# Wider warm-up matmuls, TensorE transposes for two more head tiles, and weights in K thirds in a list-scheduled head

## Chip, cores, metric

One core of one Trainium2 chip. The metric is the device time of one execution in microseconds. Kernel before: 389.12 us (median of 6 runs, 388.9 to 389.19).

## The reference

```python
x: (8, 1024, 768) f32;  gamma: (768,) f32;  w_qkv: (768, 2304) f32
rms = sqrt(mean(x**2, axis=-1) + eps)
out = matmul(x / rms * gamma, w_qkv)          # (8, 1024, 2304) f32
```

## The kernel before

The 8192 rows are 64 tiles of 128. `gamma` is folded into the weights when they are converted to bf16, `1/rms` is applied when an accumulator is evicted, so a tile needs: its load, a bf16 transposed copy `xT` (768 x 128 as six blocks), and per 512 output columns six accumulating matmuls. The first six tiles ("head") run while the weights still arrive; their order on every engine is a list of (time, operation) made in advance by a list scheduler. The rest is a loop, ordered by planned times too. Every operation is issued in that order; times only sort.

```python
PIECES = [(0, 2, 0, 512), ..., (0, 3, 512, 512), (3, 6, 512, 512), ...]   # weight loads: K chunks k0..k1, columns n0, n
LOADS  = [..., (-8.86, "x", 5), (16.69, "t", 4), (16.70, "w", 9), (21.71, "t", 5), ...]   # w piece, x tile, t: DMA transpose
HEAD_PLAN = [(4.99, "conv", 0, 0, "ACT"), ..., (5.95, "trA", 0), ..., (8.59, "mm", 0, 0, "01"), ...]
    # conv: weight chunk to bf16   trA/trB: fp32 TensorE transposes of tiles 0 to 2 (4 and 2 blocks), cpA/cpB their copies
    # tr/cp: bf16 transposes and copy (tile 3)   mm tile, column, K chunks   evac: eviction   stat, recip: row statistic

    def idle(n):                                  # warm-up matmuls
        wps = psum.tile([P, P], f32, name="pm")
        for _ in range(n):
            nc.tensor.matmul(out=wps, lhsT=warm, rhs=warm, start=True, stop=True)

    at(0.0, idle, 18)
    at(2.8, gamma_in)
    at(2.81, idle, 28)
    ...
    for t in range(HEAD, MT):                     # the steady part
        ahead = 6.0 if t < HEAD + 5 else 0.0
        at(now - 15 - ahead, load_x, t)           # unless it is in LOADS
        at(now - 8.5 - ahead, cast, t)
        at(now - 7.5 - ahead, xbar, t)            # DMA transpose of the bf16 tile into xT
        ...
```

## Time and profile before

| | before |
|---|---|
| median time | 389.12 us |
| span of the profiled run | 387.34 us |
| first real matmul starts | 8.70 us |
| last real matmul starts | 383.28 us |
| of that stretch, waits and transposes | 0.92 us, 0.34 us |

TensorE (PE in the profile) is busy nearly all the time, so whatever the other engines do is free unless TensorE waits for it. The prediction below shows the lines that say so. Times inside a run are from the start of its span. A *real* matmul is one of the product, not of the warm-up and not a transpose; a *step* is the time from the start of one to the start of the next, and it is too long by what it has over 0.216 us (0.109 us for 256 columns) and over the time of any transposes in it. The *fetch* is the transfer of a 16 KB packet of instructions, which shares the DMA engines with the loads; where no other is named, it is the first of a run. "Landed" times are those at which a load's semaphore is complete in the trace. Weight pieces are counted from 0 in the order of `PIECES`; in the kernel before piece 6 is K chunks 3 to 5 of columns 512 to 1023, in the changed kernel pieces 5, 6 and 7 share those columns, two chunks each.

### The profile page before, as it was taken

What the parts mean: (1) busy time and instruction counts of PE and PEld (TensorE: products, weight loads), DVE (VectorE), ACT (ScalarE), POOL (GpSimd) and SP (SyncE); (2) the same over time, 40 slices, a digit from 0 to 9 for tenths busy, and PEclk for the clock granted to TensorE, in tenths of its full rate; (3) what the DMA queues carried; (4) which work ended last, traced back from release to release, by engine and by line L of the source; (5) the groups of instructions that cost most, each with busy time, mean ns of one, the idle gap of its engine ahead of it and who ended that gap; (6) DMA issues with size and microseconds to landing.
All of it is one profiled execution on the core that took longest, in us unless ns stands there. A gap on an engine that the chain in (4) does not pass through costs nothing.

```text
span 387.3 us, 5554 instructions
## 1 busy us (share of the span) xinstructions
PE 381.7 (99%) x1994; PEld 194.7 (50%) x1994; DVE 153.9 (40%) x309; ACT 181.2 (47%) x362; POOL 7.5 (2%) x15
## 2 busy tenths in 40 slices
PE   8999999999999999999999999999999999999996
PEld 7444654554554554554554554554554554554552
DVE  3565524444333344333344333343333343333332
ACT  5662444443544444544444444544444534444532
POOL 0312000000000000000000000000000000000000
PEclk9999999999999999999999999999999999999999
DMA  8999999999999999999999999999999999999974
GB/s 287 390 273 389 330 361 353 372 365 323 306 289 303 311 298 317 300 297 319 292 303 303 290 328 300 296 314 292 303 274 327 322 313 287 278 352 284 307 253 182
DMA packets 89511, 119.91 MB, mean 310 GB/s; under 512 B 52358, under 2 KB 61324, under 8 KB 89484
## 3 DMA queue, kind: packets, MB, share of 16 engines
q1 hardware_dynamic: 89472, 119.56, 101.1%
q8 instruction: 15, 0.25, 0.3%
q14 instruction: 12, 0.10, 0.1%
q10 hardware_dynamic: 12, 0.00, 0.0%
HBM read 32.25 MB, written 75.50 MB: 278 GB/s over the span
## 4 chain that ended last, share of the span: by engine, by line
PE 94%; DMA 4%; POOL 0%; SPq 0%; ACT 0%; issue 0%
PE pm L229 94%; DMA w_f<-in_w_qkv_dram 3%; DMA x_t<-in_x_dram 1%; POOL w_b L168 0%; ACT ot L245 0%; SPq L158 0%; SPq L153 0%
## 5 line engine op out<-in xcount | busy, mean ns | idle before, releaser
L229 PE MATMUL pm<-w_b,xT 128*128 128x512 bf16 (+1 forms) x1920 | 374.1, 358 | 0.5 <-DVE w_b L164 0.4
L229 PEld LDWEIGHTS <-xT 128*128 128x128 bf16 x1920 | 187.7, 98 | 186.4 <-issue 1.3
L243 DVE TENSOR_SCALAR ot<-pm,rstd 128x512 f32<-128x512 f32 (+1 forms) x165 | 113.6, 693 | 201.8 <-PE pm L229 201.5
L245 ACT ACTIVATE ot<-pm,rstd 128x512 f32<-128x512 f32 (+1 forms) x155 | 100.2, 647 | 191.5 <-PE pm L229 146.6
L183 ACT ACTIVATE sq<-x_t 128x768 bf16<-128x768 f32 x64 | 53.4, 835 | 1.3 <-DMA x_t<-in_x_dram 1.2
L172 DVE CAST xb<-x_t 128x768 bf16<-128x768 f32 x61 | 33.3, 546 | 16.7 <-DMA x_t<-in_x_dram 16.7
L185 ACT ACTIVATE rms<-ssq,eps_sb 128x1 f32<-128x1 f32 x64 | 18.9, 295 | 2.1
L183 ACT ACTIVATION_READ_ACCUMULATOR sq<-x_t 128x1 f32 x64 | 12.3, 192 | 0.0
L190 DVE RECIPROCAL rstd<-rms 128x1 f32<-128x1 f32 x64 | 9.8, 154 | 3.1 <-ACT rms L185 3.1
L166 ACT ACTIVATE w_b<-w_f,g_sb 128x512 bf16<-128x512 f32 (+1 forms) x9 | 5.8, 668 | 6.1 <-DMA w_f<-in_w_qkv_dram 6.1
L168 POOL TENSOR_SCALAR w_b<-w_f,g_sb 128x512 bf16<-128x512 f32 (+1 forms) x9 | 6.8, 764 | 24.1 <-DMA w_f<-in_w_qkv_dram 24.1
L164 DVE TENSOR_SCALAR w_b<-w_f,g_sb 128x512 bf16<-128x512 f32 (+1 forms) x12 | 5.2, 450 | 4.5 <-DMA w_f<-in_w_qkv_dram 4.4
L278 PE MATMUL pm<-warm 128*128 128x128 bf16 x49 | 5.2, 294 | 1.0 <-DVE eps_sb L137 1.0
L278 PEld LDWEIGHTS <-warm 128*128 128x128 bf16 x49 | 4.7, 138 | 1.0 <-DVE eps_sb L137 1.0
L210 PE MATMUL pm<-ident_f,x_t 128*128 128x128 f32 x18 | 2.5, 278 | 0.3 <-DMA x_t<-in_x_dram 0.3
L210 PEld LDWEIGHTS pm<-ident_f,x_t 128*128 128x128 f32 x18 | 1.9, 141 | 0.7 <-PE pm L278 0.5
L172 DVE CAST xT<-pm 128x512 bf16<-128x512 f32 (+1 forms) x3 | 1.8, 592 | 0.8 <-PE pm L210 0.8
L140 ACT ACT_TABLE_LOAD x1 | 1.3, 1283 | 1.3 <-PEq L334 1.3
L174 ACT CAST xT<-pm 128x256 bf16<-128x256 f32 (+1 forms) x3 | 1.2, 445 | 0.3 <-PE pm L210 0.2
L174 ACT COPY xT<-pm 128x768 bf16<-128x768 bf16 x1 | 0.8, 798 | 0.2 <-PE pm L196 0.2
L261 DVE COPY g_sb<-pm 128x6 f32<-128x6 f32 x1 | 0.2, 164 | 1.8 <-PE pm L260 1.8
L196 PEld LDWEIGHTS <-xb 128*128 128x128 bf16 x6 | 0.4, 98 | 0.2
(13 smaller groups left out, 2.4 us busy)
## 6 DMA issues: line engine op xcount, KB each, us to landing
out_dram<-ot SPq DMA_DIRECT2D x124, 512.0 KB, 3.9
x_t<-in_x_dram SPq DMA_DIRECT2D x64, 384.0 KB, 4.3
out_dram<-ot SPq DMA_DIRECT2D x64, 128.0 KB, 3.2
w_f<-in_w_qkv_dram SPq DMA_DIRECT2D x7, 768.0 KB, 8.1
out_dram<-ot SPq DMA_DIRECT2D x8, 256.0 KB, 2.0
w_f<-in_w_qkv_dram SPq DMA_DIRECT2D x4, 256.0 KB, 6.1
xT<-xb SPq DMA_TRANSPOSE x60, 4.4
w_f<-in_w_qkv_dram SPq DMA_DIRECT2D x1, 512.0 KB, 3.9
```

What stands on the lines that cost most here:

```text
L164: nc.vector.tensor_scalar(out=o, in0=i, scalar1=g, scalar2=None, op0=mult)
L166: nc.scalar.activation(out=o, in_=i, func=AF.Copy, scale=g, bias=0.0)
L168: nc.gpsimd.tensor_scalar(out=o, in0=i, scalar1=g, scalar2=1.0, op0=mult, op1=mult)
L172: nc.vector.tensor_copy(out=out, in_=in_)
L183: nc.scalar.activation(out=sq, in_=X[t], func=AF.Square, accum_out=ssq)
L185: nc.scalar.activation(out=rms, in_=ssq, func=AF.Sqrt, scale=inv_k, bias=eps_sb)
L190: nc.vector.reciprocal(out=r, in_=RS[t])
L210: nc.tensor.transpose(out=PT[t, h][:, ko - k0, :], in_=X[t][:, ko * P:(ko + 1) * P], identity=ident_f)
L229: nc.tensor.matmul(out=PM[t, n0][:, :nl], lhsT=XT[t][:, ko, :], rhs=w_b[:, ko, n0:n0 + nl], start=(b == 1), stop=(b == KO))
L243: nc.vector.tensor_scalar(out=o, in0=pm[:, :nl], scalar1=RS[t], scalar2=None, op0=mult)
L245: nc.scalar.activation(out=o, in_=pm[:, :nl], func=AF.Copy, scale=RS[t], bias=0.0)
L278: nc.tensor.matmul(out=wps, lhsT=warm, rhs=warm, start=True, stop=True)
```

## The change

Intent: take the waits out of the head. Warm-up matmuls get 512 columns (fewer instructions for the same time), tiles 4 and 5 are transposed by TensorE and not by the DMA queue (which then never waits for a cast before it can issue the next load), the weights of columns 512 to 1535 come in thirds of K, and the list schedule is made anew for late landings. The core of the diff:

```diff
-PIECES = [..., (0, 3, 512, 512), (3, 6, 512, 512), (0, 3, 1024, 512), (3, 6, 1024, 512), ...]
+PIECES = [..., (0, 2, 512, 512), (2, 4, 512, 512), (4, 6, 512, 512), (0, 2, 1024, 512), (2, 4, 1024, 512), (4, 6, 1024, 512), ...]
 LOADS:
-    (16.69, "t", 4), (16.70, "w", 9), (21.71, "t", 5), (21.72, "w", 10), (21.73, "w", 11),
-    (21.74, "x", 6), (21.75, "x", 7),
+    (-8.85, "w", 9), (-8.84, "w", 10), (-8.83, "w", 11), (-8.82, "w", 12), (-8.81, "w", 13),
+    (-8.80, "x", 6), (-8.79, "x", 7),
 HEAD_PLAN (all of it is new; for example):
+    (14.08, "cast", 4, "DVE"), ..., (14.78, "tr", 4), ..., (15.38, "cp", 4, "DVE"), ..., (19.22, "tr", 5), ..., (19.97, "cp", 5, "DVE"),
-HEAD_END = 44.03
+HEAD_END = 44.64
-    warm = singles.tile([P, P], bf16)
+    warm = singles.tile([P, NT], bf16)
-    def idle(n):
+    def idle(n, nl=P):                            # rhs=warm[:, :nl]
-    at(0.0, idle, 18)
+    at(0.0, idle, 4, NT)
     at(2.8, gamma_in)
-    at(2.81, idle, 28)
+    at(2.81, idle, 6, NT)
+    at(2.82, idle, 3)
```

## The prediction

> **What bounds the kernel now.** I read the page first (busy shares, then the chain that ended last), then the timeline of TensorE over the first 48 us, its waits before and after 50 us, and last the DMA traffic around the two waits found. The page's group of real matmuls and the chain's stretches:
>
> ```profile
> PE 381.7 (99%) x1994; PEld 194.7 (50%) x1994; DVE 153.9 (40%) x309; ACT 181.2 (47%) x362; POOL 7.5 (2%) x15
> ...
> L229 PE MATMUL pm<-w_b,xT 128*128 128x512 bf16 (+1 forms) x1920 | 374.1, 358 | 0.5 <-DVE w_b L164 0.4
> ```
>
> ```profile
> 1.75 4.86 DMA x_t<-in_x_dram
> 6.61 0.02 issue
> 6.62 10.19 DMA w_f<-in_w_qkv_dram
> 16.82 0.08 issue
> 16.90 0.99 POOL w_b L168
> 17.89 0.04 issue
> 17.94 365.63 PE pm L229 x1883
> ```
>
> The chain (start, length) says: loads until 16.82 us, one weight conversion, then TensorE without a break to 383.57. The waits of TensorE after 50 us are an empty list. So only the head, up to 17.94, can yield anything, and the timeline of TensorE (start, length, group, idle before) says what is there:
>
> ```profile
> 3.22 2.79 PE L278 MATMUL pm<-warm 128*128 128x128 bf16 x28
> 5.84 1.68 PE L210 MATMUL pm<-ident_f,x_t 128*128 128x128 f32 x12
> 7.36 0.33 PE L278 MATMUL pm<-warm 128*128 128x128 bf16 x3
> 8.02 0.84 PE L210 MATMUL pm<-ident_f,x_t 128*128 128x128 f32 x6 [0.33 <-DMA x_t<-in_x_dram]
> 8.70 2.75 PE L229 MATMUL pm<-w_b,xT 128*128 128x512 bf16 x12
> 11.29 0.50 PE L196 MATMUL pm<-ident,xb 128*128 128x128 bf16 x6
> 11.63 5.39 PE L229 MATMUL pm<-w_b,xT 128*128 128x512 bf16 x24
> 17.38 0.38 PE L229 MATMUL pm<-w_b,xT 128*128 128x512 bf16 x1 [0.36 <-DVE w_b L164]
> 17.94 30.42 PE L229 MATMUL pm<-w_b,xT 128*128 128x512 bf16 x158 [0.18 <-POOL w_b L168]
> ```
>
> From the start times of single instructions in the trace: real matmuls follow each other at 216 ns (512 columns) and 109 ns (256). Three steps after 8.70 are longer: 265 ns at 14.0, 744 at 16.64, 555 at 17.38. Less 216 each that is 0.05 + 0.53 + 0.34 = 0.92 us. These are all the stalls there are: 1536 x 0.216 + 384 x 0.109 = 373.6 us is fixed work of a 387.3 us span. The two large ones wait for conversions of weight piece 6 (K chunks 3 to 5 of columns 512 to 1023, 768 KB), which landed at 16.82. Piece 5, the same size just ahead of it, took 2.03 us (landings at 11.67 and 13.70), piece 6 took 3.12: 1.09 more. The DMA view of 14.5 to 15.0 us shows why:
>
> ```profile
> q1 hardware_dynamic: 80, 0.19, 100.3%
> q8 instruction: 1, 0.02, 13.7%
> ```
>
> One 16 KB instruction packet starts at 14.62 and takes 1.095 us on one of the 16 DMA engines. A load lands when its slowest engine is done; all engines are saturated, so this one stays 1.09 us behind. The fetch is TensorE's: there are 15 in the run, some 25 us apart, for about 3,955 TensorE instructions, and 187 had started at the first.
>
> **What the Trainium skill says.** (1) "Runtime: NRT & Kernel Launch", Instruction fetch mechanics: instructions are fetched in 16 KiB blocks of 256, by the sequencer's own DMA queue. The trace agrees (packets of 16,384 bytes; 226 and 246 TensorE instructions between the first three), but "mostly hidden" there is not so for the load behind it. (2) "DMA: Bandwidth & Descriptors", Queues, rings and completion order: a completion counts all engines a DMA ran on. Agrees with the 1.09 us above. (3) "TensorE: Matmul & The Clock Gate", What's actually happening: the clock is released after a busy window of about 3.4 us, whatever the matmuls' number. Agrees: warm-up matmuls start 107 ns apart up to 5.43 and 56 ns apart from 5.51, after 4.5 us of activity from 0.99. (4) "VectorE: DVE Perf Modes", Why PSUM operands drop a tier: a PSUM operand allows at most two 16-bit elements per cycle. The trace before has no such VectorE copy of bf16 out of PSUM.
>
> **The change, part by part.**
>
> *Warm-up.* 49 matmuls of 128 columns become 10 of 512 and 6 of 128. Cold time of the columns: 4 x 0.427 = 1.71 us in the first group (18 x 0.107 = 1.93 before), then 6 x 0.427 = 2.56 plus three short ones (28 took 2.79). The memset is four times longer (0.11 us now, an estimate of 0.25), so TensorE starts some 0.15 us later. It still ends near 5.8, the clock is released in the same window, and the first transposes cannot start before x tile 0 lands at 5.64. Nothing on the path: 0. The hidden part is 33 x 2 = 66 TensorE instructions fewer; with 6 x 2 added for tile 4 and as many for tile 5, the 187th instruction falls just after tile 5's transposes, near 21 us.
>
> *First tiles.* The load order is unchanged up to x tile 2, which lands at 7.88 and gates TensorE at 8.02. Four of its six fp32 transposes (109 ns) now go ahead of the first real matmul, two after: it starts near 8.49 and not 8.70, the 0.22 us follow later. Sum 0.
>
> *Tiles 4 and 5 on TensorE.* 12 bf16 transposes, 56 ns each in the trace: +0.67 us, on the path, since TensorE is. The two DMA transposes that go are not on it.
>
> *Pieces in thirds.* Landings, with 2.62 us per 1,000 KB (384 KB of x took 0.98 us, 768 KB 2.03): piece 4 at 11.67 as before (same bytes ahead), piece 5 (512 KB) 13.0, x tile 4 14.0, piece 6 15.35, piece 7 16.7, x tile 5 17.7, piece 8 19.0. Now TensorE from 8.49 at 216 ns: four matmuls, two fp32 transposes, eight matmuls to 11.30; two to 11.73; tile 3's transposes to 12.07; four to 12.93; tile 3's six to 14.22; three to 14.87; tile 4's transposes to 15.2; five, then tile 4's eight, to 18.0, where piece 6 is first needed. It is converted by 16.9 (ScalarE 0.72 us, behind a row statistic of 1.3 us that waits for x tile 4): over 1 us of room, and room for a fetch too. Piece 7 is needed near 20.4, piece 8 near 25. So the 0.92 us go: -0.92.
>
> *New tight places.* By the same chaining of durations (VectorE cast 0.56, conversion 0.49, eviction 0.75; ScalarE eviction 0.65, conversion 0.72; 0.06 per semaphore): copy of tile 3 ready 12.87 against 12.93; piece 5's first chunk 14.18 against 14.22, second 14.37 against 14.44; cast of tile 4 14.95 against 14.87; copy of tile 4 16.28 against 16.38. I took 0.56 us for the PSUM copy, as the new schedule does. Margins under 0.1 us: I allow +0.15 in all.
>
> Sum: -0.92 + 0.67 + 0.15 = -0.1 us; 389.1 becomes **389.0**.
>
> **Rivals.** *VectorE becomes the wait of the head.* If its bf16 copy out of PSUM takes 0.9 us (ScalarE's took 0.80), tile 3 waits 0.3, tile 4's transposes 0.1, tile 4's matmuls 0.2: 389.5. For it: five jobs back to back between 11.7 and 16.3. Against: the two-per-cycle statement above. *The fetch does not move, or not far.* Then pieces 6 and later land 1.1 us later; piece 6 at 16.45 is converted by 17.3, still ahead of 18.0: no change of the time, which makes this rival visible only in the landings. *The clock is released one window later*, near 8.87: 16 fp32 transposes at double length put the first matmul near 9.1: +0.6, 389.7. Against: the activity starts only 0.15 us later and is denser. *Something gives way after the head.* Loads go out unbroken now, before they stopped for two DMA transposes (DMA at 35 and 165 GB/s in two slices of 1.25 us between 21 and 26), so they should end near 29 us and not 33.9, and the first stores go to the queue earlier. That can only ease the transposes of tiles 6 and 7 (landed at 42.5 and 45.3). If tile 6 were late all the same: +1 or more.
>
> **Range and chances.** Fixed work cannot shrink, so the best is about 389.1 - 0.92 + 0.67 = 388.85, less 0.3 for run and chip; the bad side adds the rivals' 0.5 to 0.7. 388.4 to 389.8. A gain of 2% is 7.8 us, more than all stalls; a loss of 2% needs a wait that nothing shows.
>
> **What would show it.** Right: no TensorE idle before piece 6's matmuls; 12 more bf16 transposes at 56 ns; the first instruction packet of 16 KB near 21 us; first real matmul near 8.5; loads over by 30 us; no waits of TensorE after 50 us. Wrong: TensorE idle between 12 and 17 us released by VectorE; warm-up matmuls still cold after 5.6; any wait beyond 30 us.

## The result

| | before | changed |
|---|---|---|
| median | 389.12 us (6 runs) | 388.69 us (6 runs, 388.5 to 388.89) |
| ratio | | 0.9991, interval 0.9978 to 1.0004 |
| span of the profiled run | 387.34 | 386.74 |
| x tile 2 landed | 7.88 | 7.75 |
| first real matmul | 8.70 | 8.35 |
| last real matmul starts | 383.28 | 382.90 |
| from x tile 2's landing to the last matmul's start | 375.40 | 375.15 |
| from there to the end of the span | 4.06 | 3.84 |
| last of the loads of the head (x tile 7) landed | 33.88 | 31.20 |

By its interval this result alone is no gain clear of the noise; the control below repeats it.

The timeline of TensorE in the changed kernel (start, length, group, and the idle time before it in brackets, where there is any):

```profile
1.19 1.89 PE L280 MATMUL pm<-warm 128*128 128x512 bf16 x4 [1.19 <-DVE eps_sb L139]
...
6.06 1.82 PE L212 MATMUL pm<-ident_f,x_t 128*128 128x128 f32 x12
...
8.35 1.03 PE L231 MATMUL pm<-w_b,xT 128*128 128x512 bf16 x4
...
12.14 2.75 PE L231 MATMUL pm<-w_b,xT 128*128 128x512 bf16 x12
14.73 0.50 PE L198 MATMUL pm<-ident,xb 128*128 128x128 bf16 x6
15.06 4.26 PE L231 MATMUL pm<-w_b,xT 128*128 128x512 bf16 x19
19.17 0.50 PE L198 MATMUL pm<-ident,xb 128*128 128x128 bf16 x6
19.50 28.70 PE L231 MATMUL pm<-w_b,xT 128*128 128x512 bf16 x147
```

No bracket stands after the first line: the waits of 0.36 and 0.18 us that stood before the matmuls at 17.38 and 17.94 are gone, and the transposes of tiles 4 and 5 stand in the row, each group pushing what follows by 0.34 us. (The matmuls at 12.14 start 0.55 us after the transposes at 11.59, where the two later groups have 0.33. The difference is one matmul whose record is missing; its weight load is on record at 11.87. This trace has 1882 of the 1920 matmuls, and every other long step without transposes in it is of exactly two matmuls.) The list of all TensorE waits of this run has one entry, the start:

```profile
PE pm L280 <- DVE eps_sb L139: 1.2, 1, 1.2
```

The chain that ended last, on the changed kernel's page, has no load in it any more, where before DMA had 4%:

```profile
PE 98%; issue 1%; ACT 0%; DVE 0%
```

The copy out of PSUM that decided a rival, from the page's groups (busy us, mean ns):

```profile
L174 DVE COPY xT<-pm 128x768 bf16<-128x768 bf16 x3 | 1.7, 557 | 0.4 <-PE pm L198 0.4
```

And the DMA view of the changed kernel from 19.5 to 20.0 us, where the first instruction packet now is (it starts at 19.59 and takes 1.09 us):

```profile
q1 hardware_dynamic: 92, 0.18, 99.3%
q8 instruction: 1, 0.02, 13.6%
```

So the span shrank by 0.60 us in this pair: 0.25 in the work from x tile 2's landing to the last matmul, 0.13 because that tile landed earlier, 0.22 after the last matmul's start.

### The profile page after: what moved, and what is told of

The parts are those of the page before. It is cut to its first block, busy times and chain, and to the rows that moved or that the text cites. A ratio compares the mean times of both kernels' runs of the same rounds, so it can differ in the third digit from the quotient of the medians.

```text
span 386.7 us, 5481 instructions
## 1 busy us (share of the span) xinstructions
PE 380.0 (98%) x1935; PEld 193.1 (50%) x1973; DVE 157.0 (41%) x316; ACT 180.5 (47%) x360; POOL 4.6 (1%) x12
## 4 chain that ended last, share of the span: by engine, by line
PE 98%; issue 1%; ACT 0%; DVE 0%
PE pm L231 96%; PE pm L280 1%; PE pm L212 1%; PE pm L198 0%; ACT ot L247 0%; DVE warm L135 0%; PE pm L262 0%; DVE eps_sb L139 0%
## 5 line engine op out<-in xcount | busy, mean ns | idle before, releaser
L166 DVE TENSOR_SCALAR w_b<-w_f,g_sb 128x512 bf16<-128x512 f32 (+1 forms) x15 | 6.8, 486 | 4.5 <-DMA w_f<-in_w_qkv_dram 4.4
L280 PE MATMUL pm<-warm 128*128 128x512 bf16 (+1 forms) x16 | 5.3, 493 | 1.2 <-DVE eps_sb L139 1.2
L170 POOL TENSOR_SCALAR w_b<-w_f,g_sb 128x512 bf16<-128x512 f32 (+1 forms) x6 | 3.9, 652 | 25.3 <-DMA w_f<-in_w_qkv_dram 25.3
L280 PEld LDWEIGHTS <-warm 128*128 128x128 bf16 x16 | 1.8, 131 | 3.4 <-issue 2.2
L174 DVE CAST xT<-pm 128x256 bf16<-128x256 f32 (+1 forms) x5 | 2.4, 527 | 1.9 <-PE pm L212 1.9
L174 DVE COPY xT<-pm 128x768 bf16<-128x768 bf16 x3 | 1.7, 557 | 0.4 <-PE pm L198 0.4
L198 PEld LDWEIGHTS <-xb 128*128 128x128 bf16 x18 | 1.3, 98 | 0.7
L198 PE MATMUL pm<-ident,xb 128*128 128x128 bf16 x18 | 1.5, 219 | 0.0
```

What stands on the lines that cost most here:

```text
L166: nc.vector.tensor_scalar(out=o, in0=i, scalar1=g, scalar2=None, op0=mult)
L170: nc.gpsimd.tensor_scalar(out=o, in0=i, scalar1=g, scalar2=1.0, op0=mult, op1=mult)
L174: nc.vector.tensor_copy(out=out, in_=in_)
L280: nc.tensor.matmul(out=wps[:, :nl], lhsT=warm[:, :P], rhs=warm[:, :nl], start=True, stop=True)
```

## The experiments

Twelve runs: ten edited kernels, and both kernels once more. "B" stands for the kernel before with an edit, "A" for the changed kernel with one. The diffs are cut to their core: B with another warm-up also has `idle` with its second argument and the `warm` tile of 512 columns, whose memset is longer (0.27 us, 0.11 before), so that TensorE starts at 1.19 us and not at 0.99. To set apart what differs from run to run, I use the time from x tile 2's landing to the last matmul's start: the landing itself moved between 7.59 and 8.81 us over the profiled runs.

### b_wide: B with the new warm-up alone

```diff
-    warm = singles.tile([P, P], bf16)
+    warm = singles.tile([P, NT], bf16)
-    at(0.0, idle, 18)
+    at(0.0, idle, 4, NT)
-    at(2.81, idle, 28)
+    at(2.81, idle, 6, NT)
+    at(2.82, idle, 3)
```

> Kernel before with the new warm-up alone (10 matmuls of 512 columns and 6 of 128 in place of 49 of 128); pieces, schedule and DMA transposes of tiles 4 and 5 as before. Theory (the stalls at 16.6 to 17.9 us come from the instruction fetch that falls into weight piece 6; fewer TensorE instructions move it): first 16 KB instruction packet near 21.7 us (66 instructions, 33 matmuls of 216 ns after 14.6), piece 6 lands near 15.7, no wait of TensorE longer than 0.1 us after the first real matmul, no transposes added: 0.85 us less than before, near 388.25, so 0.4 less than the changed kernel. Rival (the thirds and the new order remove the stalls): piece 6 still lands near 16.8, the waits of 0.5 and 0.3 us stay, 389.1.

Measured: 389.57 us against 389.03 before, ratio 1.0017 (1.0005 to 1.0030): slower by its interval, where 0.85 us less was expected. The first half of the theory held: the fetch moved to 20.58 us, piece 6 landed at 15.75, and no real matmul waits before 22 us. But two other waits came. TensorE's timeline of this run, about 23 and about 76 us:

```profile
19.75 3.19 PE L229 MATMUL pm<-w_b,xT 128*128 128x512 bf16 x14
23.38 6.87 PE L229 MATMUL pm<-w_b,xT 128*128 128x512 bf16 x31 [0.45 <-DMA xT<-xb]
```

```profile
71.81 2.11 PE L229 MATMUL pm<-w_b,xT 128*128 128x512 bf16 x12
76.01 2.33 PE L229 MATMUL pm<-w_b,xT 128*128 128x512 bf16 x9 [2.08 <-DMA xT<-xb]
```

Both wait for a DMA transpose. The first is tile 4's: issued at 17.4, behind 2 MB of loads in the queue and with the fetch at 20.58 before it; the step there is 0.61 us too long. The second is tile 11's, long after the head. This profiled run was the slowest of the six (391.02); the others were 389.23 to 389.66, so the wait of over 2 us is not typical of them.

### a_narrow: A with the old warm-up

```diff
-    at(0.0, idle, 4, NT)
+    at(0.0, idle, 18)
-    at(2.81, idle, 6, NT)
-    at(2.82, idle, 3)
+    at(2.81, idle, 28)
```

> Changed kernel with the old warm-up (49 matmuls of 128 columns). Theory: the fetch comes back to about 15.3 us (66 TensorE instructions earlier), just after piece 6 has landed, and pieces 7 and 8 and x tile 5 land 1.1 us later (17.6, 19.9, 18.6), but they are needed later still: no wait of TensorE, time as the changed kernel within 0.2 us (388.7). So the new pieces and order are enough by themselves against this fetch, as the new warm-up is by itself. Rival (the warm-up's instruction count is what removes the waits, or the wide warm-up is worth something by itself): 0.5 us or more above the changed kernel.

Measured: 388.99 us (388.89 to 389.32), ratio 0.9999. As the theory had it, the fetch came at 15.19, pieces 7 and 8 and x tile 5 landed at 17.78, 20.14 and 18.77 (16.47, 18.81 and 17.46 in the changed kernel), and TensorE had no wait but the start. From x tile 2 to the last matmul 375.28 us, 0.13 more than the changed kernel. The median is 0.2 above that kernel's control on the same chip, at the edge of what was allowed: the first real matmul came at 8.72, since its 46 cold matmuls of 128 columns ended at 6.38 us, 0.32 later than the 13 of the changed kernel, which have 384 columns fewer in all. So the new pieces and order bear the fetch by themselves.

### b_dose: B with 12 TensorE instructions fewer

```diff
-    at(2.81, idle, 28)
+    at(2.81, idle, 2, NT)
+    at(2.82, idle, 20)
```

> Kernel before with only 8 of its 49 warm-up matmuls replaced by 2 of 512 columns: same cold time, 12 TensorE instructions fewer. Theory: the fetch moves by 6 matmuls of 216 ns, to about 15.9 us, just behind piece 6's landing near 15.7, so the waits at 16.6 to 17.9 vanish although next to nothing has changed: 388.3 (0.8 less than before). x tile 4 and later land 1.1 us late as before. Rival (the wide warm-up acts by itself, by the clock or by density): with a fifth of it the gain is a fifth or nothing, 389.0.

Measured: 389.19 us (388.54 to 389.47), ratio 1.0001: no gain. The fetch came at 16.54, piece 6 landed at 15.34, and the waits at 16.6 to 17.9 are gone, in which the theory was right. But I had overlooked that piece 7 then lands 1 us late (19.29) and is needed near 19.2: a step 0.25 us too long at 19.38 in this run, 0.60 in the later run of the same head. The delay does not go away, it goes to the next load. A second loss is of another kind: in this run the clock was released only at 7.07 us, TensorE was still at its earlier work when x tile 2 landed, and the first real matmul came 1.26 us after that landing (0.82 in the kernel before). And tile 11's transpose landed at 73.58, and the weight load that needs it stands at 73.62: no matmul was late yet, but nothing was left. The profiled run was the fastest of the five (388.54), so it does not show what the slower ones lost.

### a_tr2: A with the transposes of tiles 4 and 5 made twice

```diff
     def tr(t):
-        for ko in range(KO):
+        for ko in [k for _ in range(2 if t in (4, 5) else 1) for k in range(KO)]:
```

> Changed kernel with the transposes of tiles 4 and 5 made twice (the same values written again). Theory: TensorE is on the path, 12 more at 56 ns are 0.67 us: 389.35, the changed kernel plus 0.67. Rival (the transposes run beside waits that TensorE has anyway): plus 0.1 or less.

Measured: 389.55 us (389.29 to 389.86), against 388.79 of the changed kernel on the same chip: +0.76 in the medians; from x tile 2 to the last matmul 375.82 against 375.15, +0.67. In its timeline the groups of six have become twelve and nothing gives way:

```profile
14.75 0.83 PE L198 MATMUL pm<-ident,xb 128*128 128x128 bf16 x12
15.42 4.26 PE L231 MATMUL pm<-w_b,xT 128*128 128x512 bf16 x19
```

The term of +0.67 us is thus measured by doubling it.

### after_again and before_again: both kernels once more

> The changed kernel once more, as control on this chip. Theory: 0.3 to 0.5 us below the kernel before (388.6 to 388.8); no wait of TensorE after the first real matmul; the moment of the clock's release another than 6.7 us after the span's start, since it moved between 4.3 and 7.2 us over the runs so far, and the first real matmul between 8.3 and 8.8 with it. Rival (the first result was luck of the run): same as before within 0.1.

Measured: 388.79 us against 389.06 before on this chip, ratio 0.9993 (0.9980 to 1.0006), 0.27 less: just under what was expected. Two runs give the same sign and neither interval excludes 1. The profiled run was this kernel's slowest (389.19): x tile 2 landed at 8.32, yet from there to the last matmul it took 375.15 us, to the hundredth as in the first run. The clock's release was at 4.15 us. The first real matmul came at 8.92, later than the 8.3 to 8.8 expected, because x tile 2 was late.

> The kernel before once more, one look. Theory: the fetch near 14.6 to 15.0 us and piece 6 at 16.5 to 16.9 again, TensorE waiting 0.5 to 1.0 us in all before 18 us; the clock's release at another moment than 5.46. Rival (the two waits were of that one run): no wait over 0.1 us between 16 and 18 us.

Measured: 388.83 us in the one run. The fetch came at 14.64. But piece 6 landed in time (15.59), x tile 4 0.95 us late (17.53), piece 7 at 19.57, and TensorE waited for piece 7's conversion:

```profile
11.63 7.93 PE L229 MATMUL pm<-w_b,xT 128*128 128x512 bf16 x35
20.13 1.24 PE L229 MATMUL pm<-w_b,xT 128*128 128x512 bf16 x5 [0.57 <-DVE w_b L164]
```

The step is 0.74 us too long, where the first run lost 0.87 in two. So with the fetch at the same time (14.62 and 14.64) the load that it made late differed; both runs lost 0.7 to 0.9 us in the head. The expectation named only one of the places and missed there. It also makes the gain of the change smaller than the first pair says: from x tile 2 to the last matmul this run takes 375.22 us, only 0.07 more than the changed kernel.

### b_wide4: B with the new warm-up and tile 4 on TensorE

```diff
-    (16.69, "t", 4), (16.70, "w", 9), ...
+    (16.70, "w", 9), ...
-    ..., (18.06, "recip", 4),
+    ..., (18.06, "recip", 4), (18.08, "tr", 4), (18.20, "cp", 4, "DVE"),
```

and the warm-up of b_wide.

> Kernel before with the new warm-up and with tile 4 alone transposed by TensorE (six transposes and one VectorE copy; tile 5 still by DMA). The run of the new warm-up alone had no wait for piece 6, but one of 0.61 us at 22.6 us for tile 4's DMA transpose, which stands in the queue behind 2 MB of loads and behind the fetch at 20.6. Theory (that wait took the place of the one removed, and TensorE transposes of tile 4 are what takes it away): no wait of TensorE over 0.1 us between 9 and 30 us, cost 0.34 us for six transposes: 0.5 us below the kernel before, near 388.5. Rival (the loss of the warm-up alone lies elsewhere, in the start or in the steady part): 389.2 or more.

Measured: 389.32 us with a wide spread (388.55 to 390.02), ratio 1.0010. No wait between 9 and 30 us, as expected: TensorE transposes take tile 4's wait away. Yet the time did not follow. In the profiled run tile 11's transpose landed at 73.74 and was used at 73.78, and the step there is 0.27 us too long. That made tile 11 the suspect. It is the first tile whose load, cast and DMA transpose are ordered without the lead of 6 us (`ahead`). Over the runs so far (times from the traces; "used" is the start of the weight load that needs the tile, some 0.1 us before its first matmul where nothing waits; "waited" is by how much the step is too long, which is a little more than the idle time in the brackets above):

| run | last load of the head | tile 11 landed | tile 11 used | room |
|---|---|---|---|---|
| before | 33.88 | 73.43 | 74.03 | 0.60 |
| before_again | 33.99 | 73.44 | 73.85 | 0.41 |
| b_dose | 33.83 | 73.58 | 73.62 | none |
| b_wide4 | 33.08 | 73.74 | 73.78 | none, waited 0.27 |
| b_wide | 34.34 | 75.97 | 76.01 | none, waited 2.25 |
| changed | 31.20 | 71.42 | 73.65 | 2.23 |
| after_again | 30.89 | 72.40 | 74.22 | 1.82 |
| a_narrow | 31.05 | 71.15 | 74.02 | 2.87 |

In the kernel before, tile 11 has less room (0.41 to 0.60 us) than the head loses (0.74 to 0.92). Save the loss in the head, and TensorE comes to tile 11 too early. In the changed kernel the loads of the head are over 2.7 us sooner, the first store is issued at 22.83 us (27.03 before), and there is room. But the end of the head's loads does not order the whole table: in b_wide4 they end 0.8 us sooner than in the kernel before, and tile 11 lands 0.3 later. A rival for part of the lateness is the third fetch, which the warm-up's count moves too: it came at 61.19 before, and in b_wide at 69.53, while tile 11's transpose was under way; that transpose took 6.5 us from its issue to its landing, where the runs of this table with no fetch starting inside it had 4.6 to 5.7. No run parts the two.

### a_first: A with two matmuls ahead of tile 2's transposes

```diff
-    (7.26, "idle", 3), (7.32, "cpA", 0, "ACT"), ...
-    (7.94, "trA", 2), ..., (8.37, "mm", 0, 0, "01"),
+    (7.32, "cpA", 0, "ACT"), ...
+    (7.93, "mm", 0, 0, "01"), (7.94, "trA", 2), ...
```

> Changed kernel with the first two real matmuls (tile 0) ahead of tile 2's transposes, and without the three warm-up matmuls there. Theory: what TensorE still loses is before its first real matmul; two matmuls (0.43 us) fill the time in which it waits for x tile 2 or runs the three warm-ups: 0.2 us (late clock) to 0.4 us (early clock) below the changed kernel, near 388.4. Rival (copies of tile 0 or the release of accumulators gate these two matmuls): no gain.

Measured: 388.70 us against 388.79: nothing that can be told from the spread (388.53 to 389.21). The two matmuls did start early:

```profile
7.33 0.61 PE L231 MATMUL pm<-w_b,xT 128*128 128x512 bf16 x2
8.01 0.66 PE L212 MATMUL pm<-ident_f,x_t 128*128 128x128 f32 x4
8.51 0.59 PE L231 MATMUL pm<-w_b,xT 128*128 128x512 bf16 x2
8.94 0.38 PE L212 MATMUL pm<-ident_f,x_t 128*128 128x128 f32 x2
9.46 2.33 PE L231 MATMUL pm<-w_b,xT 128*128 128x512 bf16 x10
```

but a step 0.30 us too long now stands before the matmuls at 9.46, those of tile 2. 374.98 us from x tile 2 to the last matmul is 0.17 less than the changed kernel; the rival, that something gates them, was nearer, though later in the row than it said.

### b_dose_ahead, b_wide_ahead, b_wide4_ahead: the lead for tiles 11 to 13

```diff
-        ahead = 6.0 if t < HEAD + 5 else 0.0
+        ahead = 6.0 if t < HEAD + 8 else 0.0
```

> The 12-instruction warm-up change on the kernel before, and tiles 11 to 13 loaded, cast and transposed 6 us earlier in the order of the queue (one number in the loop). Finding behind it: tile 11 is the first whose DMA transpose is ordered without that lead; in the kernel before it landed at 73.4 us and was used at 74.0 and 73.85, in the first run of this warm-up at 73.58 with use at 73.62, in the wide warm-up at 75.97 with use at 75.97, with a wait of 2.2 us. Theory (what is saved in the head is given back at tile 11, because the queue is still behind from the head): with the lead it lands by 71, no wait near 74 us, 0.5 to 0.8 us below the kernel before: 388.3 to 388.6, and the spread of the runs is as narrow as that kernel's. Rival (tile 11 is one chance event; the medians of the two runs are set elsewhere): 389.1 to 389.2 as without it.

> The new warm-up alone on the kernel before, with the same lead for tiles 11 to 13. Theory: the wait of 0.6 us for tile 4's DMA transpose at 22.6 us stays, the wait at tile 11 goes: 0.5 to 0.9 us below the 389.55 without the lead, near 388.8. Rival: 389.5.

> The new warm-up and tile 4 on TensorE on the kernel before, with the same lead for tiles 11 to 13. Theory: no wait of TensorE after the first real matmul at all (without the lead two waits of 0.27 and 0.23 us near 73.4 in the profiled run, more in others): near 388.5, 0.8 below the 389.32 without the lead. Rival: 389.3.

Measured on another chip, where the kernel before took 389.13 us:

| run | without the lead | with it | ratio with it |
|---|---|---|---|
| b_dose | 389.19 | 388.98 (388.80 to 389.10) | 0.9998 (0.9984 to 1.0011) |
| b_wide | 389.57 | 388.87 (388.55 to 389.14) | 0.9994 (0.9982 to 1.0007) |
| b_wide4 | 389.32 | 388.47 (388.30 to 388.84) | 0.9985 (0.9972 to 0.9997) |

Tile 11 has 1.9 us of room or more in the two runs that have its landing on record (b_dose_ahead 69.88 against a use at 73.83; b_wide_ahead 71.92 against 73.86, though a fetch at 69.09 fell into this transpose too and it took 7.3 us). None of the three waits after 24 us (the 0.23 us that the expectation of b_wide4_ahead reads near 73.4 beside the 0.27 is a missing record: the weight loads there stand at 73.78, 73.80 and 74.02), and their spreads are narrow again. b_wide and b_wide4 fell by 0.70 and 0.85 us, as the theory said; since these pairs ran on different chips, the ratios to the kernel before are the surer measure: 1.0017 to 0.9994 and 1.0010 to 0.9985. With the lead, b_dose did not reach the expected 388.3 to 388.6. Its head still waits for piece 7, where the step is 0.60 us too long, and its first real matmul came 0.15 us later after x tile 2 than in the kernel before:

```profile
20.12 30.10 PE L229 MATMUL pm<-w_b,xT 128*128 128x512 bf16 x157 [0.44 <-DVE w_b L164]
```

In b_wide_ahead x tile 2 landed late (8.51), so TensorE came to tile 4 late enough to wait only 0.10 us; the 0.6 us that were expected to stay there did not show in this run, and no other profile of it is on record.

b_wide4_ahead is the fastest version and its interval excludes 1. Its timeline has all 1920 matmuls on record and, after the start, no wait:

```profile
8.48 2.75 PE L229 MATMUL pm<-w_b,xT 128*128 128x512 bf16 x12
11.07 0.50 PE L196 MATMUL pm<-ident,xb 128*128 128x128 bf16 x6
11.41 6.64 PE L229 MATMUL pm<-w_b,xT 128*128 128x512 bf16 x30
17.88 0.50 PE L196 MATMUL pm<-ident,xb 128*128 128x128 bf16 x6
18.22 32.16 PE L229 MATMUL pm<-w_b,xT 128*128 128x512 bf16 x169
```

From x tile 2 to the last matmul it takes 374.82 us, 0.33 less than the changed kernel, as much as the six transposes of tile 5 take that it leaves to the DMA queue. It and the changed kernel were not run on the same chip; by ratio to the kernel before they stand at 0.9985 and 0.9991 to 0.9993, with intervals that overlap.

### b_early: B with 92 TensorE instructions more

```diff
-    at(0.0, idle, 18)
+    at(0.0, idle, 36, 64)
-    at(2.81, idle, 28)
+    at(2.81, idle, 56, 64)
```

> The other direction: the kernel before with its two warm-up groups as 36 and 56 matmuls of 64 columns in place of 18 and 28 of 128, the same columns in 92 TensorE instructions more. Theory (the fetch goes with the count of TensorE instructions): the first 16 KB packet comes during the warm-up, near 5 to 6 us and not at 14.6; x tiles 1 or 2 land about 1 us later (x tile 2 near 8.8), the first real matmul near 9.7; piece 6 or x tile 4 is then late by the same 1 us but TensorE too, so no wait of 0.5 us between 16 and 20 us; all in all 0 to 0.6 us above the kernel before. Rival (the fetch comes by time, or other traffic delays piece 6): packet near 14.6 us and waits of 0.7 to 0.9 us between 16 and 20 us again.

Measured: 392.03 us (391.09 to 393.62), ratio 1.0080 (1.0063 to 1.0098), where 0 to 0.6 us more were expected. The fetch did go with the count and not with the clock on the wall: it came at 9.34 us, and the second at 31.47 where the kernel before has it at 39.85; 9.34 is later than I had worked out. By the records of the traces 225 TensorE instructions had started by then; in the other thirteen profiled runs 182 to 207 had at the first fetch, at times from 14.62 to 20.95 us. So the count sets it only roughly. x tile 2 landed at 8.81 and the first real matmul was at 9.63, as expected, but the tile was late before that packet started, so the fetch is not shown to be the cause of it. No wait of 0.5 us between 16 and 20 us, as expected. What I missed is the second fetch: it falls on the last weight piece, which landed at 33.90 (31.68 before), the last load at 35.85, and the queue was still behind at tiles 11 and 12:

```profile
75.73 6.01 PE L229 MATMUL pm<-w_b,xT 128*128 128x512 bf16 x30 [0.83 <-DMA xT<-xb]
82.41 7.95 PE L229 MATMUL pm<-w_b,xT 128*128 128x512 bf16 x39 [0.67 <-DMA xT<-xb]
```

This is the table of tile 11 from its other end: the loads of the head end 2 us later, and tiles 11 and 12 make TensorE wait although it was itself 0.9 us late.

## Why the prediction was right

It said 389.0 us (388.4 to 389.8), the same within 2%; measured were 388.69 and, in the control, 388.79. Point by point:

- *The two waits go (-0.92).* Right in size: no wait is left in any profiled run of the changed kernel or of those that keep its pieces and schedule, except before the first matmuls. Their cause is the fetch: it goes with the number of TensorE instructions (a_narrow, b_dose, b_wide), and in the five runs in which it came between 14.6 and 16.6 us a load behind it is 0.9 to 1.1 us late. The 16 updates of a load's semaphore, one for each DMA engine, show that one engine is held: of piece 6 in the kernel before, fifteen had landed by 15.72 us and the last at 16.82; pieces 7 and 8 behind it still have their last 0.96 and 0.93 us after the fifteenth, where pieces 4 and 5 ahead of it have 0.12. In the changed kernel the same happens where nothing waits for it: pieces 10 to 13 have their last engine 1.5 us late, pieces 4 to 8 0.1. (The page that the prediction's point 2 names says that a completion counts engines, but in the section "Why a DMA increments its semaphore by 16 and not by 1".) The prediction tied the wait to piece 6; before_again showed that it can be piece 7 with a somewhat smaller loss (0.74), so the 0.92 is the size of one run.
- *Twelve transposes (+0.67).* Right: a_tr2 measured 0.67 when they were doubled.
- *New tight places (+0.15).* Not needed: TensorE has no wait there. The copy out of PSUM took 557 ns, as assumed, so the rival of a waiting VectorE did not come about. Without this allowance the sum is -0.25, and 375.40 to 375.15 us from x tile 2 on is -0.25. That the two agree to the hundredth belongs to this pair: against before_again it is -0.07.
- *Warm-up worth 0.* Right for the time, with one reason wrong. The clock's release does not stay "in the same window": it came at 5.46 us before and at 6.75 in the changed kernel, and anywhere from 4.15 to 7.22 over all profiled runs. In the changed kernel's run the first fp32 transposes were thus still at 213 ns; TensorE was done with its warm-up at 7.88, 0.13 us after x tile 2 had landed, so it cost next to nothing. The prediction also read 4.5 us from the start of activity to the release as agreement with a window of 3.4; over all profiled runs it was 2.96 to 6.03 us, so that agreement was one of a single run. The narrow warm-up of a_narrow, 0.32 us longer when cold, lost 0.13.
- *The fetch near 21 us.* It came at 19.59: I had counted rows of a listing that puts several fp32 transposes into one. By the trace 201 TensorE instructions, not 187, had started at the fetch of the kernel before, and 200 in the changed kernel; the page counts 3,988 in all, not 3,955. It lands behind piece 8 either way.
- *Loads over by 30 us.* The last landed at 31.20. Right in kind, 1.2 us off, and the fetch is why: fifteen of its DMA engines were done at 29.70, the last 1.50 us later.
- *"That can only ease the transposes of tiles 6 and 7".* Right in sign, but it missed the place that matters. This is the part of the change that the prediction undervalued: not the head, but tile 11 at 74 us, had 0.4 to 0.6 us of room, and a version that saves the head's waits without making room there gives much of it back (b_wide, b_wide4; the lead restored 0.7 and 0.85 us). For b_dose this is not shown: its wait for piece 7 and its late start account for what its lead run missed. I read the empty list of waits after 50 us as room; an empty list only says that room is not negative.

The rest of the difference between the two profiled runs is outside this sum: 0.13 us is x tile 2 landing earlier in that run (in the control it landed 0.57 later, so it is not from the change as far as these runs show), and 0.22 us lies after the last matmul's start. There the kernel before has an 8 KB packet of another queue at 385.70 us, beside its last store, and the changed kernel has it at 382.39, ahead of it. The runs derived from the changed kernel have 3.83 to 3.85 us there, those from the kernel before 3.93 to 4.06, so some 0.1 to 0.2 us goes with the kernel. That the packet is the cause was not tested.

What stays open: why x tile 2's landing moves by a microsecond from run to run, and how much of the spread of the times that is; and how much of the changed kernel's tile 11 room comes from the two DMA transposes taken out of the head, how much from loads issued without a break, and how much from earlier stores, since no run parts them; and why the same fetch made piece 6 late in one run and piece 7 in another.

## What to carry to other kernels

When the bound engine has no wait after some point, measure the room of each later hand-over (landing to use) before counting a saving ahead of it; what is saved can come back as a wait where the room is smallest, here at the first tile without a lead. A load that lands late by about a microsecond may have an instruction fetch in front of it on one DMA engine: look whether one of the 16 semaphore updates is late, count the instructions up to it, and move the need for the load rather than the fetch, which in b_dose only hit the next load. And doubling a suspected cost is a cheap test of whether it is on the path.

## What the Trainium skill lacked or had wrong

- "Runtime: NRT & Kernel Launch", Instruction fetch mechanics, calls the cost of a block boundary mostly hidden. For instruction issue that agrees: b_wide4_ahead has all 1920 matmuls on record and 15 fetches, and after 8.48 us its only long steps are the two with transposes in them. What it lacks is the load behind it: one 16 KB packet took 1.0 to 1.1 us in these heads, and the last DMA engine of a load behind it landed 0.9 to 1.1 us after the fifteenth (piece 6 before 15.72 and 16.82; piece 7 in a_narrow 16.74 and 17.78, in b_dose 18.37 and 19.29).
- "TensorE: Matmul & The Clock Gate", What you observe, gives the release at about 4 us of activity, within 500 ns. Here activity began at 1.0 to 1.2 us and the release came between 4.15 and 7.22 us, 2.96 to 6.03 us after it, a spread of 3 us. The same page (What's actually happening) has a free-running window of about 3.4 us; a whole busy window would then end 3.4 to 6.8 us after the start, an estimate from the page's figure. The late releases fit that, the earliest (2.96 in after_again, 3.11 in a_tr2) do not.
- "VectorE: DVE Perf Modes", Why PSUM operands drop a tier, was right where it decided something: 768 bf16 columns out of PSUM took 557 ns, while ScalarE took 798.
- I found no page that says how long a DMA transpose may stand behind other traffic: tile 11's landed 5.2 us after its issue in the kernel before (68.2 to 73.43) and 6.5 us in b_wide (69.5 to 75.97).
